# Modulation products in the mixer's gaps, a mean inside the last slab and a shorter routing chain, in a two-block network

## The chip, the cores and the metric

One core of one Trainium2 chip runs one program. The metric is the device time of one execution in microseconds (us). The engines named are PE (TensorE, matmuls), DVE (VectorE), ACT (ScalarE), POOL (GpSimd) and SP (SyncE, which only issues DMAs here).

## The reference

A first block on x (256 tokens x 1024) in float32, then a second block of four layers (swiglu, RWKV, Mamba and windowed attention). The change lies in the first block:

```
mod = (silu(c) @ w_ada + b_ada).reshape(bsz, 6, d)       # 6 x 1024 numbers: "ada1"; the second block has 72 chunks of 512, "ada2"
sh1, sc1, g1, sh2, sc2, g2 = [mod[:, j, None, :] for j in range(6)]
u = modulate(x, sh1, sc1)                                # normalise, * (1 + sc1) + sh1
mix = hybrid_mixer(u, ...)                               # rg_lru and attention, concatenated, @ w_out
x = layernorm(ALPHA * x + g1 * mix, ln1_g, ln1_b)
u2 = modulate(x, sh2, sc2)
ffn = hierarchical_moe(u2, ...)
x = layernorm(ALPHA * x + g2 * ffn, ln2_g, ln2_b)
# hierarchical_moe: 4 groups of 8 experts of width 256
g_top, g_idx = top_k(softmax(xc @ w_rg + b_rg), 1)
e_in = the 8 logits of that group
e_top, e_loc = top_k(softmax(e_in), 2); e_top = e_top / sum(e_top)
weights = g_top * e_top                                  # two experts for each token
y = sum over the two: weight * ((silu(x @ w1) * (x @ w3)) @ w2)
```

## The kernel before

Activations lie with the 1024 features on partitions, as eight tiles of 128 x 256 tokens (J = 8). A float32 matmul runs as three: each weight tile (1 MB, 128 x 2048, loaded by SP into one of four "raw" buffers, L315) is split by ACT into hi (L326) and by DVE into lo (L327), and hi*high, lo*high and hi*low are summed (mm3, L337). A raw buffer is free for the next load once lo, or what else reads it, is done; SP issues its loads in one fixed order.

Chunks of the modulation (512 numbers, two loads each) are made beside the main work, in two ways. On PE (gemv): "acc" matmuls with silu(c) as the stationary operand, a copy to "rows" on ACT, small "c" matmuls that turn the row into a column, an addition on DVE (L407). On DVE (gemv_v, L425): four products a chunk, each a 128 x 1024 multiplication by silu(c) (laid out in a tile cb by silu_rows) with a sum along the row, and a last addition of the bias (L429). ON_VECTOR says which chunks go which way. pump(n) does n PE chunks, pump(n, True) n DVE chunks, pump_parts yields after every product, need(key) does what is due.

The first block runs in this order. hybrid(): first norm, projections (the h matmuls), the recurrence and the attention (u0 to u3 by "gathered": scores, softmax with its divisions on POOL, L1356 and L1357, transposes), then the output in four slabs of w_out, out(0) to out(3) (y matmuls), the last ending tile by tile in the residual (L529). moe(): layernorm and modulate, each one call of centred: mean by eight matmuls with a constant ("bm"), U = x - mean (L576, DVE), squares on ACT (L517), their sum "st" by PE, root in ten small DVE steps (L466 to L476), broadcast "bc" by PE; then "ut" (L558, DVE) and the affine part on ACT (L560). Then router logits ("pl", lg at L1676), transposes of U ("ut" on PE) to tokens tokh and tokl, and the routing: maxima, one-hot choices, softmaxes, "own" (which of eight slots of pairs of experts a token takes), its running count "pr", "rank", one-hot matrices Gm, their transposes GT ("gt"), the gather "pg" of tokens (gh, gl), the weights "pge", and the experts' matmuls ("eh", "yp", "ya" for the scatter). mosti is the largest count of a slot; a second pass follows if it is over 128 (it isn't).

The scheduler orders each engine's instructions by priority in the order of the code; `with self.ordered()` fixes the order within a piece. silu(c1) is loaded twice before, and moe's two norms hold four chunks by `more()`:

```
more = lambda: self.pump(1, True)
with self.ordered():
    self.modulate(U, self.centred(U, more), self.col("ln1_g"), self.col("ln1_b"), self.x)
```

Of the kernel before, what the change touches and what calls it, by code (L numbers as in the profile page):

```python
# [10 lines left out]
F32 = mybir.dt.float32  # L11
# [15 lines left out]
ON_VECTOR = {"ada1": (0, 1, 2, 3, 6, 7, 8, 9), "ada2": range(2, 72)}  # L27
# [241 lines left out]
class Program:  # L269
    def __init__(self, ctx, tc, a, out):  # L270
# [4 lines left out]
        self.raw = e(tc.tile_pool(name="raw", bufs=4))  # L275
# [13 lines left out]
        self.vf = None  # L289
# [23 lines left out]
    def load(self, name, i):  # L313
        t = self.raw.tile([P, 2048], F32, name="raw")
        self.nc.sync.dma_start(t, self.a[name][i])  # L315
        return t
# [29 lines left out]
    def tr(self, out, in_, ident=None):  # L346
        self.nc.tensor.transpose(out, in_, self.k("ident") if ident is None else ident)
# [70 lines left out]
    def gemv_v(self, name, chunk, bias, out):  # L418

        nc = self.nc  # L420
        for h in range(2):
            r = self.load(name, 2 * chunk + h)
# [130 lines left out]
    def modulate(self, src, bc, A, sh, dst=None, follow=None):  # L553

        nc = self.nc
        for m in range(J):
            t = self.t1("ut")
            self.last = nc.vector.scalar_tensor_tensor(t, src[:, m, :], A[:, m:m + 1], bc, op0=OP.mult, op1=OP.mult)  # L558
            if dst is not None:
                nc.scalar.activation(dst[:, m, dst.shape[2] - T:], t, AF.Identity, bias=sh[:, m:m + 1])  # L560
                if follow:
                    follow.tile(m)
                continue
# [4 lines left out]
    def centred(self, xc, between=None):  # L568

        nc = self.nc  # L570
        bm = self.bank([P, T], "bm", self.st_tag)
        for m in range(J):
            self.mm(bm, self.k("mean"), self.x[:, m, :], m == 0, m == J - 1)
# [4 lines left out]
        if between:  # L578
            self.last = last
            with self.ordered():  # L580
                between()
            with self.ordered():
                return self.bcast_t(self.rsqrt(st, 1.0 / D, 1e-5, 2))
        return self.bcast_t(self.rsqrt(st, 1.0 / D, 1e-5, 2))
# [864 lines left out]
    def hybrid(self):  # L1449
# [3 lines left out]
        with ExitStack() as ctx:  # L1453
# [11 lines left out]
            self.silu_rows("c1", ar.tile([P, D], F32, name="cb1", tag="Z", bufs=1))  # L1465
# [7 lines left out]
            self.new_u()  # L1473
            self.modulate(xc, bc, A, M[:, 0:8])
# [108 lines left out]
            for m in range(4):  # L1583
                t = self.t1("lo")
                stt(t, cv[:, m, :], self.col("norm_lru_g", m, 1), bc, op0=OP.mult, op1=OP.mult)
                self.split(m, t)
            self.st_tag = "m"
            ys = [self.bank([P, 2, T]) for _ in range(4)]

            def out(s):  # L1590
                w = self.slab("w_out", s)
                for kk in range(2):
                    for m in range(J):
# [20 lines left out]
            out(2)  # L1614
            self.pump(1)
            out(3)
            self.st_tag = "y"


    def moe(self, follow, cb):  # L1620
# [3 lines left out]
        with ExitStack() as ctx:  # L1624
# [9 lines left out]
            nc.sync.dma_start(rb, bass.AP(tensor=rbd.tensor, offset=rbd.offset, ap=[[0, P], [1, 36]]))  # L1634
            wr = self.load("router", 0)
            U = arr("U", [P, J, T], tag="big")
            self.silu_rows("c1", ar.tile([P, D], F32, name="cb1", tag="tokh"))
            more = lambda: self.pump(1, True)
            with self.ordered():
                more()  # L1640
            with self.ordered():
                self.modulate(U, self.centred(U, more), self.col("ln1_g"), self.col("ln1_b"), self.x)
            with self.ordered():
                more()
            with self.ordered():
                bc = self.centred(U, more)
            self.need((0, 2))
            self.silu_rows("c2", cb)
            A = self.consts.tile([P, J], F32, name="A", bufs=2)
            ts(A, M[:, 32:40], 1.0, None, op0=OP.add)  # L1650
            self.modulate(U, bc, A, M[:, 24:32], U)
            for m in range(J):
                act(self.x[:, m, :], self.x[:, m, :], AF.Copy, scale=ALPHA)
# [7 lines left out]
            with self.tc.issue_after(last.ins):  # L1661
                self.pump(3)
            with self.ordered():
                more()
            tokh, tokl = arr("tokh", [P, 2, 1024], dt=F32R), arr("tokl", [P, 2, 1024], dt=F32R)
            for k in range(J):
# [5 lines left out]
                tt(tokl[:, :, c], pt, tokh[:, :, c].bitcast(F32), op=OP.subtract)  # L1672
            new = lambda name, shape: arr("r_" + name, [P, 2] + shape)
# [3 lines left out]

            def softmax(t, n, name):
                mx = new("mx" + name, [1])
                red(mx, t, axis=AX.X, op=OP.max)  # L1680
                tt(t, t, bcv(mx, n), op=OP.subtract)
                act(t, t, AF.Exp)
                red(mx, t, axis=AX.X, op=OP.add)
                nc.vector.reciprocal(mx, mx)
                tt(t, t, bcv(mx, n), op=OP.mult)
# [11 lines left out]
            softmax(lg[:, :, 0:4], 4, "g")  # L1697
            gtop, og = first_max(lg[:, :, 0:4], 4, "g")
# [9 lines left out]
            ge, sw, hh = new("ge", [8]), new("sw", [1]), new("hh", [2])  # L1708
            tt(ei, o1, o2, op=OP.add)
            red(hh, ei.rearrange("p c (h e) -> p c h e", h=2), axis=AX.X, op=OP.max)  # L1710
            tt(sw, e1, e2, op=OP.add)
# [219 lines left out]
```

## Time and profile before

| what | value |
|---|---|
| median of 3 runs | 3105.38 us (3096.54 to 3112.08) |
| the profiled execution | 3116.96 us, span 3115.1 us, mean granted clock 0.952 |
| PE busy | 2940.8 us, 94% |
| DVE, ACT, POOL busy | 74%, 52%, 6% |
| L425 products | 312, mean 1221 ns |
| chain that ended last | PE 70%, DVE 6%, ACT 3% |

A row of a timeline tells when an instruction started, how long it ran, and in brackets how long its engine had been idle before and for whom it waited. A row with x8 joins eight of one kind. Matmuls in float32 show two records for each in a row such as bm x16 (two passes), so counts of records are not always counts of instructions.

### The profile page before, as it was taken

How to read it: one execution, taken by the hardware profiler on the slowest of the kernel's cores; microseconds unless marked ns; L12 is line 12 of the kernel's file. 1: busy time of each engine (PE TensorE's matmuls, PEld its weight loads, DVE VectorE, ACT ScalarE, POOL GpSimd, SP SyncE). 2: the span in 40 equal slices, each digit the busy share in tenths (PEclk: the TensorE clock that was granted, in tenths of full speed). 3: DMA queues.
4: the chain of work that ended last, by engine and by line, in shares of the span. 5: the costliest groups of instructions: out<-in, count | busy, mean ns of one | idle time of the engine just before them, and what ended most of it. 6: DMA issues, size and time to landing. Idle time of an engine off the chain costs nothing.

```text
span 3115.1 us, 57344 instructions
## 1 busy us (share of the span) xinstructions
PE 2940.8 (94%) x23191; PEld 2721.9 (87%) x23191; DVE 2297.2 (74%) x4064; ACT 1612.9 (52%) x2779; POOL 187.1 (6%) x244
## 2 busy tenths in 40 slices
PE   7979999799889999999899999999899999899999
PEld 6867888699768899999899999997899998777899
DVE  6668888677685787776887777767776876855754
ACT  5537777444544444544775545445644544542543
POOL 1200000000410000000000000001200001400000
PEclk8979999799889999999999999999999999898999
DMA  8468888476133378584554785863487682213353
GB/s 305 167 250 324 323 324 324 180 296 257 68 113 133 132 277 323 207 316 154 199 195 157 290 293 210 322 230 138 175 298 277 241 310 95 108 60 131 147 180 135
DMA packets 95192, 674.45 MB, mean 217 GB/s; under 512 B 10759, under 2 KB 12104, under 8 KB 14664
## 3 DMA queue, kind: packets, MB, share of 16 engines
q1 hardware_dynamic: 94920, 670.71, 57.8%
q8 instruction: 184, 3.01, 0.4%
q14 instruction: 88, 0.72, 0.1%
HBM read 666.95 MB, written 3.72 MB: 215 GB/s over the span
## 4 chain that ended last, share of the span: by engine, by line
PE 70%; DVE 6%; ACT 3%; POOL 1%; issue 1%; DMA 0%; POOLq 0%; DVEq 0%; ACTq 0%; SPq 0%
PE h L337 40%; PE y L337 16%; PE ea L337 3%; DVE lo L327 1%; PE pk L337 1%; PE py L337 1%; PE st L337 1%; ACT hi L326 1%; PE pg L337 1%; PE pw L337 1%; PE hb L337 1%; DVE ut L558 1%; PE z L337 1%; PE zg L337 1%; PE pa L337 1%
## 5 line engine op out<-in xcount | busy, mean ns | idle before, releaser
L327 DVE TENSOR_TENSOR lo<-raw,hi 128x1024 fp32r<-128x1024 f32 x897 | 1085.2, 1226 | 375.4 <-ACT hi L326 372.5
L326 ACT CAST hi<-raw 128x1024 fp32r<-128x1024 f32 x897 | 928.1, 1050 | 634.3 <-PE h L337 284.9
L337 PE MATMUL h<-uh,hi 128*128 128x256 f32 x3552 | 1023.6, 288 | 20.2 <-ACT hi L326 11.6
L337 PE MATMUL h<-uh,lo 128*128 128x256 f32 x3552 | 1016.5, 287 | 11.4 <-DVE lo L327 11.4
L337 PE MATMUL h<-ul,hi 128*128 128x256 f32 x3552 | 1016.8, 286 | 9.0 <-DVE ul L358 9.0
L337 PEld LDWEIGHTS h<-uh,hi 128*128 128x128 f32 x3552 | 682.9, 192 | 32.8 <-ACT hi L326 14.0
L337 PEld LDWEIGHTS h<-uh,lo 128*128 128x128 f32 x3552 | 682.6, 192 | 16.1 <-DVE lo L327 13.2
L337 PEld LDWEIGHTS h<-ul,hi 128*128 128x128 f32 x3552 | 683.2, 192 | 14.4 <-DVE ul L358 10.4
L425 DVE SCALAR_TENSOR_TENSOR raw<-raw,cb 128x1024 f32<-128x1024 f32 x312 | 375.1, 1221 | 42.2 <-DMA raw<-in_ada 41.7
L337 PE MATMUL y<-gh,hi 128*128 128x256 f32 x1408 | 395.7, 281 | 0.0
L337 PE MATMUL y<-gh,lo 128*128 128x256 f32 x1408 | 395.6, 281 | 0.0
L337 PE MATMUL y<-gl,hi 128*128 128x256 f32 x1408 | 395.5, 281 | 0.0
L337 PEld LDWEIGHTS y<-gh,hi 128*128 128x128 f32 x1408 | 265.6, 189 | 0.0
L337 PEld LDWEIGHTS y<-gl,hi 128*128 128x128 f32 x1408 | 265.5, 189 | 0.0
L337 PEld LDWEIGHTS y<-gh,lo 128*128 128x128 f32 x1408 | 265.1, 188 | 0.0
L521 POOL TENSOR_TENSOR sq<-sq 128x256 f32<-128x256 f32 x60 | 49.5, 824 | 2234.0 <-ACT sq L517 1705.5
L357 ACT CAST gh<-g 128x256 fp32r<-128x256 f32 x176 | 71.3, 406 | 155.1 <-DVE g L627 151.0
L625 ACT ACTIVATE sa<-h 128x256 f32<-128x256 f32 x160 | 60.8, 380 | 140.6 <-PE h L337 140.0
L337 PE MATMUL eh<-hi,gh 128*128 128x512 f32 x256 | 104.5, 408 | 0.7 <-ACT hi L326 0.7
L337 PE MATMUL eh<-lo,gh 128*128 128x512 f32 x256 | 103.2, 403 | 1.8 <-DVE lo L327 1.8
L337 PE MATMUL eh<-hi,gl 128*128 128x512 f32 x256 | 101.9, 398 | 0.0
L337 PE MATMUL ea<-uh,hi 128*128 128x258 f32 x312 | 89.9, 297 | 2.0 <-ACT uh L221 2.0
(489 smaller groups left out, 4266.3 us busy)
## 6 DMA issues: line engine op xcount, KB each, us to landing
raw<-in_ffn_in SPq DMA_DIRECT2D x176, 1024.0 KB, 4.9
raw<-in_ada SPq DMA_DIRECT2D x168, 1024.0 KB, 5.1
raw<-in_w SPq DMA_DIRECT2D x96, 1024.0 KB, 4.8
raw<-in_ffn_out SPq DMA_DIRECT2D x88, 1024.0 KB, 7.1
raw<-in_rw SPq DMA_DIRECT2D x32, 1024.0 KB, 4.8
raw<-in_mb_in SPq DMA_DIRECT2D x24, 1024.0 KB, 4.9
raw<-in_w_in SPq DMA_DIRECT2D x10, 1024.0 KB, 5.5
raw<-in_mb_out SPq DMA_DIRECT2D x8, 1024.0 KB, 4.7
```

Source lines behind the costliest of these rows:

```text
L326: self.nc.scalar.copy(hi, r[:, c])
L327: self.nc.vector.tensor_tensor(lo, r[:, c], hi.bitcast(F32), op=OP.subtract)
L337: self.pe = self.nc.tensor.matmul(out, lhs, rhs, start=start, stop=stop, skip_group_check=True)
L357: self.nc.scalar.copy(uh[:, m, :], t)
L425: nc.vector.scalar_tensor_tensor(w, w, 1.0, self.cb, op0=OP.mult, op1=OP.mult, accum_out=out[:, 2 * h + j:2 * h + j + 1])
L521: self.nc.gpsimd.tensor_tensor(self.acc, self.acc, sq, op=OP.add)
L558: self.last = nc.vector.scalar_tensor_tensor(t, src[:, m, :], A[:, m:m + 1], bc, op0=OP.mult, op1=OP.mult)
L625: nc.scalar.activation(sa, a, AF.Silu, bias=bias)
```

## The change

- ada2 chunks 0 and 1 go from PE to DVE. Of the DVE chunks due in moe, five (ada1 6 to 9, ada2 0) are made in hybrid() as single products at eleven places, `some(n)`; ada2 1 to 3 in moe as 12 single products. The four products at the experts' end are gone. silu(c1) stays in the permanent tile; loads of these chunks in moe go to two buffers of their own ("side"). The PE chunks ada1 10 and 11 go to between the norms and behind the token transposes.
- The mean's matmuls of the first norm stand inside out(3), two tiles behind the residual. The factor ALPHA on x goes into the affine step (L560) and the next norm's constants.
- own is made from the raw logits; softmax weights (`weights`) and the largest count (`count`) are made beside the first gather. GT comes after the gather; gl of the first gather is cast on DVE. SP's load of the count stands earlier.

```diff
-ON_VECTOR = {"ada1": (0, 1, 2, 3, 6, 7, 8, 9), "ada2": range(2, 72)}
+ON_VECTOR = {"ada1": (0, 1, 2, 3, 6, 7, 8, 9), "ada2": range(72)}
...
+    def mean_of(self, m):
+        if m == 0:
+            self.bm = self.bank([P, T], "bm", self.st_tag)
+        if m >= 0:
+            self.mm(self.bm, self.k("mean"), self.x[:, m, :], m == 0, m == J - 1)
...
+            ahead = self.pump_parts(5)
...
             project(2)
             S[2] = weigh(2)
+            some(1)
             gathered(0, S[0])
             project(3)
+            some(2)
             S[3] = weigh(3)
+            some(1)
             gathered(1, S[1])
+            some(1)
...
                         if s == 3 and kk == 1:
                             self.residual(m, y, M[:, 16:24], None)
+                            self.mean_of(m - 2)
...
-            out(0)
+            out(0, 2)
             gathered(2, S[2])
             self.pump(1)
-            out(1)
+            out(1, 3)
             gathered(3, S[3])
             self.pump(1)
+            some(3)
...
-            out(2)
-            self.pump(1)
-            out(3)
+            out(2, 2)
             self.st_tag = "y"
+            self.silu_rows("c2", ar.tile([P, D], F32, name="cb2", tag="zr", bufs=1))
+            some(2)
+            out(3, 2)
...
+            self.modulate(U, self.centred(U, lambda: some(3)), self.col("ln1_g"), ab, self.x, scale=ALPHA)
+            self.pump(1)
+            with self.ordered():
+                some(3)
+            self.modulate(U, self.centred(U, lambda: (some(3), self.flush()), ALPHA), A, M[:, 24:32], U)
+            with self.ordered():
+                some(3)
...
-            softmax(lg[:, :, 0:4], 4, "g")
-            gtop, og = first_max(lg[:, :, 0:4], 4, "g")
+            gmax, og = first_max(lg[:, :, 0:4], 4, "g")
...
-            softmax(ei, 8, "e")
             e1, o1 = first_max(ei, 8, "1")
-            stt(ei, o1, -2.0, ei, op0=OP.mult, op1=OP.add)
+            stt(ei, o1, -3e38, ei, op0=OP.mult, op1=OP.add)
...
-                    nc.scalar.copy(gl[:, k], pg[:, 1])
+                    (nc.vector.tensor_copy if start else nc.scalar.copy)(gl[:, k], pg[:, 1])
+                if start:
+                    weights()
+                    mosti.append(count())
```

What the order of the instructions makes of it. First DVE from the last residuals to the first norm's root, before (mod_91 is ada1's result, mod_87 ada2's):

```order
L529 SCALAR_TENSOR_TENSOR x<-y,mod_91,x 128x256 x8
L407 TENSOR_TENSOR mod_91<-c_1571,cols 128x4
L425 SCALAR_TENSOR_TENSOR raw,mod_91<-raw,cb_1568 128x1024 x4
L429 TENSOR_TENSOR mod_91<-mod_91,cols 128x4
L576 TENSOR_TENSOR U<-x,bm 128x256 x8
L425 SCALAR_TENSOR_TENSOR raw,mod_91<-raw,cb_1568 128x1024 x4
L429 TENSOR_TENSOR mod_91<-mod_91,cols 128x4
L466 TENSOR_SCALAR rsv<-st 128x2
```

and after:

```order
L529 SCALAR_TENSOR_TENSOR x<-y,mod_91,x 128x256
L429 TENSOR_TENSOR mod_87<-mod_87,cols 128x4
L529 SCALAR_TENSOR_TENSOR x<-y,mod_91,x 128x256 x6
L1675 TENSOR_SCALAR ab<-cols 128x8
L1676 TENSOR_SCALAR A<-mod_91 128x8
L529 SCALAR_TENSOR_TENSOR x<-y,mod_91,x 128x256
L577 TENSOR_TENSOR U<-x,bm 128x256 x8
L425 SCALAR_TENSOR_TENSOR raw,mod_87<-raw,cb 128x1024 x2
L466 TENSOR_SCALAR rsv<-st 128x2
L467 TENSOR_SCALAR rst<-rsv 128x2
L468 TENSOR_SCALAR rsy<-rst 128x2
L470 TENSOR_TENSOR rst<-rsy 128x2
```

Two of the chunks' products stood in front of U by fours; now U follows the last residual, and two products stand behind it, a third within the root (behind the last row shown, L472).

DVE in the mixer, from the second unit's scores to the first root, before:

```order
L1354 RECIPROCAL sm<-sm 128x4
L1577 TENSOR_TENSOR cv<-cv,yg 128x256
L1348 TENSOR_SCALAR nm<-nm 128x4
L1577 TENSOR_TENSOR cv<-cv,yg 128x256
L327 TENSOR_TENSOR lo<-raw,hi 128x1024
L1354 RECIPROCAL sm<-sm 128x4
L327 TENSOR_TENSOR lo<-raw,hi 128x1024
L1577 TENSOR_TENSOR cv<-cv,yg 128x256 x2
L327 TENSOR_TENSOR lo<-raw,hi 128x1024
```

and after:

```order
L425 SCALAR_TENSOR_TENSOR raw,mod_91<-raw,cb 128x1024
L1356 TENSOR_SCALAR nm<-nm 128x4
L1595 TENSOR_TENSOR cv<-cv,yg 128x256 x2
L425 SCALAR_TENSOR_TENSOR raw,mod_91<-raw,cb 128x1024
L1362 RECIPROCAL sm<-sm 128x4
L327 TENSOR_TENSOR lo<-raw,hi 128x1024
L425 SCALAR_TENSOR_TENSOR raw,mod_91<-raw,cb 128x1024
L1362 RECIPROCAL sm<-sm 128x4
L425 SCALAR_TENSOR_TENSOR raw,mod_91<-raw,cb 128x1024
L1595 TENSOR_TENSOR cv<-cv,yg 128x256 x2
L429 TENSOR_TENSOR mod_91<-mod_91,cols 128x4
L327 TENSOR_TENSOR lo<-raw,hi 128x1024
```

Three lo of weight slabs stood between the attention's steps; now two, and four products (one more chunk's stand further ahead).

PE behind the last accumulation to the gather, before:

```order
L337 MATMUL acc<-raw,s_c_85 32x512 x8
L337 MATMUL c_1879<-kc,rows 128x1 x4
L337 MATMUL pr<-r_own,kc 128x8 x5
L347 MATMUL gt<-kc,Gm 128x128 x4
L337 MATMUL pg<-Gm,tokh 128x256 x2
L337 MATMUL pg<-Gm,tokl 128x256 x2
```

and after:

```order
L337 MATMUL acc<-raw,s_c_83 32x512 x8
L337 MATMUL pr<-r_own,kc 128x8 x3
L337 MATMUL pg<-Gm,tokh 128x256 x3
L337 MATMUL pg<-Gm,tokl 128x256 x2
L337 MATMUL pg<-Gm,tokh 128x256
L337 MATMUL pg<-Gm,tokl 128x256 x2
L337 MATMUL eh<-hi,gh 128x512
L337 MATMUL pg<-Gm,tokh 128x256 x2
L337 MATMUL pg<-Gm,tokl 128x256 x2
```

gt stood in front of the first pg; now pg follows pr, and the first expert matmuls (eh) stand among the pg.

## Rows read from the trace of the kernel before

**Rows 1.** Windows: stretch, busy PE, PEld, DVE, ACT, POOL, clock, DMA, GB/s.

```profile
100.00:120.00 20.00, 18.60 (x149) 16.45 (x148) 13.21 (x26) 17.42 (x35) 14.36 (x13) 1.00 0.34 116
...
400.00:420.00 20.00, 20.00 (x106) 16.93 (x105) 19.00 (x27) 13.62 (x19) 0.00 (x0) 1.00 0.78 278
```

**Rows 2.** Finer windows, after the mixer's last matmul and in the first norm.

```profile
169.00:175.00 6.00, 1.92 (x9) 1.33 (x8) 5.96 (x14) 0.45 (x2) 0.00 (x0) 1.00 0.36 127
...
175.00:182.00 7.00, 6.83 (x32) 6.75 (x32) 6.62 (x16) 2.28 (x7) 0.00 (x0) 0.52 0.73 277
```

**Rows 3.** Timeline of PE: start, us, op, tiles, count, idle before.

```profile
160.47 0.39 PE L337 MATMUL y<-uh,hi 128*128 128x256 f32 x1
...
168.48 0.28 PE L337 MATMUL y<-uh,lo 128*128 128x256 f32 x1
...
168.59 2.32 PE L337 MATMUL bm<-x,kc 128*128 128x256 f32 x10
...
175.02 6.83 PE L337 MATMUL st<-kc,sq 128*128 128x1 f32 x32 [4.10 <-ACT sq L517]
...
193.51 5.34 PE L337 MATMUL st<-kc,sq 128*128 128x1 f32 x32 [2.52 <-ACT sq L517]
...
210.84 0.91 PE L337 MATMUL pl<-raw,U 128*128 128x36 f32 x4
...
223.23 1.94 PE L337 MATMUL acc<-raw,s_c 128*32 128x512 f32 x8 [0.76 <-DMA raw<-in_ada]
...
227.60 2.28 PE L337 MATMUL pr<-r_own,kc 128*128 128x8 f32 x10
...
230.62 1.24 PE L347 MATMUL gt<-kc,Gm 128*128 128x128 f32 x4 [0.74 <-DVE mosti L1734]
...
231.78 0.80 PE L337 MATMUL pg<-Gm,tokh 128*128 128x256 f32 x2
...
249.11 0.39 PE L337 MATMUL eh<-lo,gh 128*128 128x512 f32 x1
```

**Rows 4.** Timeline of DVE: norms and routing.

```profile
169.26 1.22 DVE L425 SCALAR_TENSOR_TENSOR raw<-raw,cb 128x1024 f32<-128x1024 f32 x1
...
174.04 2.73 DVE L576 TENSOR_TENSOR U<-x,bm 128x256 f32<-128x256 f32 x8
...
184.69 3.22 DVE L558 SCALAR_TENSOR_TENSOR ut<-U,cols,bc 128x256 f32<-128x256 f32 x8 [0.86 <-PE bc L347]
...
192.60 2.73 DVE L576 TENSOR_TENSOR U<-x,bm 128x256 f32<-128x256 f32 x8
...
198.68 1.22 DVE L425 SCALAR_TENSOR_TENSOR raw<-raw,cb 128x1024 f32<-128x1024 f32 x1
...
202.88 3.22 DVE L558 SCALAR_TENSOR_TENSOR ut<-U,A,bc 128x256 f32<-128x256 f32 x8 [0.92 <-PE bc L347]
...
211.83 0.22 DVE L1676 TENSOR_TENSOR r_lg<-pl,rb 128x72 f32<-128x72 f32 x1
...
225.29 0.17 DVE L1722 TENSOR_TENSOR r_own<-r_og,r_hh 128x16 f32<-128x16 f32 x1
```

**Rows 5.** Timeline of ACT, end of the first gather.

```profile
238.64 0.38 ACT L1756 CAST gl<-pg 128x256 fp32r<-128x256 f32 x1
```

**Rows 6.** Timeline of POOL and DVE in the mixer's attention.

```profile
98.44 0.93 POOL L1357 TENSOR_SCALAR S<-S,sm 128x256 f32<-128x256 f32 x1
...
102.22 1.22 DVE L327 TENSOR_TENSOR lo<-raw,hi 128x1024 fp32r<-128x1024 f32 x1
...
102.23 2.00 POOL L1357 TENSOR_SCALAR S<-S,sm 128x256 f32<-128x256 f32 x1
```

**Rows 7.** Timeline of SP: DMA issues near the mixer's last weight slab.

```profile
146.30 0.33 SPq L315 DMA_DIRECT2D raw<-in_w_out  x1
```

**Rows 8.** Timeline of DVE and PE at the experts' end.

```profile
551.85 1.22 DVE L425 SCALAR_TENSOR_TENSOR raw<-raw,cb 128x1024 f32<-128x1024 f32 x1
...
553.53 0.77 PE L337 MATMUL ya<-GT,yhl 128*128 128x256 f32 x4 [2.78 <-DVE x L529]
```

More of the change, by code (lines that the diff above doesn't have):

```diff
@@ L421, in gemv_v @@
         for h in range(2):
-            r = self.load(name, 2 * chunk + h)
+            r = self.load(name, 2 * chunk + h, self.side)
             for j in range(2):
@@ L566, in modulate, with centred @@
                                            op0=OP.add, op1=OP.subtract)
-    def centred(self, xc, between=None):
+    def centred(self, xc, between=None, scale=1.0):
         nc = self.nc
-        bm = self.bank([P, T], "bm", self.st_tag)
-        for m in range(J):
-            self.mm(bm, self.k("mean"), self.x[:, m, :], m == 0, m == J - 1)
+        for m in range(0 if self.bm is None else J, J):
+            self.mean_of(m)
+        bm, self.bm = self.bm, None
         st = self.stat()
@@ L1473, in hybrid, with some @@
             self.new_u()
+            ahead = self.pump_parts(5)
+            def some(n):
+                for _ in range(n):
+                    next(ahead)
             self.modulate(xc, bc, A, M[:, 0:8])
@@ L1586, in hybrid, with out @@
                 self.split(m, t)
+            some(1)
             self.st_tag = "m"
             ys = [self.bank([P, 2, T]) for _ in range(4)]
-            def out(s):
+            def out(s, then=0):
                 w = self.slab("w_out", s)
+                some(then)
                 for kk in range(2):
@@ L1660, in moe, with tokens @@
                                    k == 0 and th == 0, k == J - 1)
[L1661 to L1664, printed above, removed]
             tokh, tokl = arr("tokh", [P, 2, 1024], dt=F32R), arr("tokl", [P, 2, 1024], dt=F32R)
-            for k in range(J):
+            def tokens(k):
                 pt = self.bank([P, 2, P], "ut", "h")
@@ L1723, in moe @@
                hh[:, :, None, :].to_broadcast([P, 2, 4, 2]), op=OP.mult)
-            pr = self.bank([P, 3, 8], "pr", "m")
+            for k in range(J):
+                tokens(k)
+            with self.tc.issue_after(self.tr_last.ins):
+                self.pump(1)
+            pr = self.bank([P, 2, 8], "pr", "m")
             tri, ones = self.k("mtri")[:, 0:P], self.k("ones")
@@ L1728, in moe, with count, weights, gather @@
             self.mm(pr[:, 1, :], tri, own[:, 1, :], False, True)
[L1729 to L1736 removed]
+            self.last = nc.vector.tensor_copy(rank, pr)
+            mosti = []
+            def count():
+                pm = self.bank([P, 8], "pm", "m")
+                self.mm(pm, ones, own[:, 0, :], True, False)
+                self.mm(pm, ones, own[:, 1, :], False, True)
+                most, n = arr("most", [P, 1]), arr("mosti", [P, 1], dt=I32)
+                red(most, pm, axis=AX.X, op=OP.max)
+                nc.vector.tensor_copy(n, most)
+                return n
+            def weights():
+                lgg = lg[:, :, 0:4]
+                tt(lgg, lgg, bcv(gmax, 4), op=OP.subtract)
+                act(lgg, lgg, AF.Exp)
+                tt(e2, e2, e1, op=OP.subtract)
+                act(e2, e2, AF.Exp)
+                red(e1, lgg, axis=AX.X, op=OP.add)
+                ts(sw, e2, 1.0, None, op0=OP.add)
+                tt(e1, e1, sw, op=OP.mult)
+                nc.vector.reciprocal(e1, e1)
+                tt(e2, e2, e1, op=OP.mult)
+                tt(o1, o1, bcv(e1, 8), op=OP.mult)
+                tt(o2, o2, bcv(e2, 8), op=OP.mult)
+                tt(ge, o1, o2, op=OP.add)
+            def gather(g, start=False):
                 Gm, GT = arr("Gm", [P, 2, 2, P], dt=F32R), arr("GT", [P, 2, T], 2, F32R)
@@ L1820, in experts @@
                     ts(rank, rank, -128.0 * window, None, op0=OP.add)
-                G, later, hd, GT = gather(0), None, None, None
+                G, later, hd, GT = gather(0, not window), None, None, None
                 for e in range(33):
@@ L1852, in moe @@
             self.need((0, 3))
-            count = nc.values_load(mosti[0:1, 0:1], min_val=0, max_val=T)
-            with self.tc.If(count > P):
+            most = nc.values_load(mosti[0][0:1, 0:1], min_val=0, max_val=T)
+            with self.tc.If(most > P):
                 experts(1)
+            self.side = None
             self.st_tag = "m"
```

100 lines of the change are left out of this document (38 added, 62 removed).

## The prediction

> **What bounds the kernel now.** I read the windows first. In [rows 1] the columns to see are PE's busy time and the clock. The experts (400 to 420 us) keep PE busy for 20.00 of 20 us at clock 1.00: that stage is as long as its matmuls, and nothing the change does before it shortens it; it can only begin earlier. The mixer at 100 to 120 us is nearly as full on PE (18.60), while DVE has 13.21 busy there: some room for products, if they can be slipped in without making PE wait. What lies between is different: in [rows 2] a PE that waits, and a clock of 0.52 (mostly the lower level) when it works again at 175 us, after the idle 169 to 175. From the end of the last mixer matmul (168.48 + 0.28 = 168.76 us, T0 below) to the 24th expert matmul (249.11 + 0.39 = 249.50, second and last rows of [rows 3]) 80.7 us pass in which one chain of small steps sets the end. The chain of waits as a view reaches back only to the branch behind the experts, so I followed this stretch by hand through PE and DVE [rows 3, 4].
>
> Sums are made against the profiled execution (3116.96 us); the median of the three runs is 3105.38, 11.6 us lower, and I carry the difference over to it.
>
> **Norms: products out, mean in the slab.** Before, four products (1.15 us apart) run between the residual and U, four beside the statistics, four between the norms, four in the second norm, 16 in all [rows 4]. U waits for the first four: it starts at 174.04, T0 + 5.28, though the mean's matmuls end at 168.59 + 2.32 = 170.9. After, the order has U right behind the last residual, and all but the last mean matmuls stand in front of the last y: one residual (about 0.4) and some four mean matmuls (0.23 each by the ten of [rows 3]) give U at about T0 + 1.25. The products that remain are 12: two between U and the root, one within the root (its ten steps are 0.2 us apart, so that one costs its whole 1.15), three before the second U, and the same again, with the last three before the logits.
> From U to ut it was 10.65 us (174.04 to 184.69); statistics at 6.83 us for 32 at the lower level. Since PE now idles only some 3 us before them they may run faster: if they merely follow the squares, ut comes at T0 + 10.3; if as before, with the extra product, at T0 + 13.2. I take 11.6. To the second U: 3.22 for ut, three products instead of four, so 6.75 instead of 7.91: T0 + 18.4 (before 23.84). Second norm: the products no longer end after the statistics (before 198.68 + 1.2 = 199.9 against 193.51 + 5.34 = 198.85, 1.1 us), one stands in the root (+1.15): 10.3 as before (192.60 to 202.88), ut at T0 + 28.7. From there to the logits (8.95 before) PE is the limit: pl with transposes between, to 210.84 + 0.91; fewer transposes come in between, and the three products that stand in front of lg fit under it. 8.2: logits at T0 + 36.9, before 43.07. Saved 6.2; from 3.5 (lower level in both norms) to 9.5 (upper level in both).
>
> **Routing.** From logits to own it was 13.6 us (211.83 to 225.46). Four chained softmax parts, of which two exponentials on ACT, and waits for c matmuls and tokl's casts on DVE go out. After, about 21 steps 0.2 us apart (4.65 with the wider ones) and eight tokl subtractions (0.34 each) that DVE takes in between, plus some wait for tokh: 8.1 us. From own to the first gather matmul it was 6.3 us (225.46 to 231.78): c, pr x10 in 2.28, rank, Gm, then gt x4 in 1.24 in front of pg [rows 3]. After: pr has six of ten passes (1.4), gt is behind, all four Gm must be there: 4.5. The eight remaining acc matmuls stand before pr (1.94 for such a group) but lie beside the DVE chain. Saved 13.6 + 6.3 - 8.1 - 4.5 = 7.3. If ACT's hi of the second weight slab, which now sits between tokh's casts, waits for its load, 2 us of it are lost.
>
> **Gather to the 24th expert matmul.** Before 17.7 (231.78 to 249.50): all of pg, then pge, then 24 eh, the first of them with a wait for lo. After, gt (1.24) and a second small count fall into this stretch, but eh stand among pg as soon as a gh is there; the eight casts of gl go from ACT (0.38 each [rows 5], 3.0 in all) to DVE, which has lost four products there, so that hi and lo come sooner. If none of that helps it is 17.7 + 1.24 + 1.3 for the count and the longer queue, 20.2; if ACT's 3.0 and the waits for the first eh go, and gt fits into gaps, 15.5. I take 17.0: saved 0.7 (from -2.5 to +2.2). SP's new place for the count (a register load after six expert loads instead of at the end) has 90 expert loads queued behind it; the count is ready with the first gather, before the seventh of these loads can have a free buffer, so I put it at nothing; if that cover fails, each us of lateness is one of PE's.
> Sum of the stretch: 6.2 + 7.3 + 0.7 = 14.2 saved, from 9 to 19.
>
> **Mixer.** It takes 20 products (23 us of DVE) and their ten 1 MB loads more, and loses one group of acc on PE in front of the last slab (-1.9). Eight of them lie before the first root, where DVE is fullest: 9.2 us against the 6.8 that DVE has left from 100 to 120 us and some before 100. And they meet POOL: its 128x256 step takes 0.93 alone and 2.00 when it starts with a lo on DVE (102.23 and 102.22 in [rows 6]), 1.07 more. A product has lo's shape and time. Four stand between the attention's steps (the order of DVE in the mixer shows it), in place of one of three lo: at 1.07 each POOL's chain is some 3 to 4 us longer, of which PE waits for a part only since the slab's h matmuls are there to fill.
> The Trainium skill (SBUF — State Buffer, "SBUF: two separate sides") says that a DVE instruction with two SBUF inputs and a GpSimd instruction that reads SBUF exclude one another for the whole instruction; the 2.00 against 0.93 agrees. By that rule all four products cost POOL a full 1.1 us each, 4.3 together; if products were harmless there the mixer's term would be about 2 us smaller.
> Then a lo between the second root and its use (+1.2) and the last slab's load, issued at 146.30 before [rows 7], now with two more 1 MB loads close to it; y of that slab starts at 160.47 (the first row of [rows 3]), 14.2 us after the issue, so a few us of lateness are covered. Together the mixer is 3.5 us longer; bounds -2 (all hidden, acc gone) and +8 (POOL's 4.3, lo's 1.2, DVE's 2.4 too much).
>
> **Tail.** Four products, the last at 551.85, stand between the last steps of the experts and the residuals: PE's ya waits 2.78 for DVE [rows 8]. Without them the residuals begin 2.1 us earlier, and two small steps (0.3) go: -2.4, bounds -1 and -2.8. The second block's own work is not touched.
>
> **Sum.** -14.2 + 3.5 - 2.4 = -13.1: 3103.9 against the profiled run, 3092.3 against the median. I say 3092; its own range is 3084 to 3099.
>
> **Rivals.** (A) The clock: fewer idle us let the norms and the gather run at the upper level. For it: 1.00 at 169 to 175 [rows 2], so the level falls only after the wait for U, and that wait shrinks from 4.10 (behind the statistics) by more than half. Against: pl, small transposes and one-column statistics keep gaps between them. Then -19 + 2 - 2.4, about -19: 3086. (B) The mixer gives it back: the PE there is full, each late root or late slab goes to the end one for one, and the stretch saves its lower 9: -9 + 8 - 1, about -2: 3103. (C) Slower than before: the four raw buffers. The chunks' loads stand in SP's order in front of the mixer's slabs, and a load waits until a product has freed a buffer; the product waits its turn on DVE behind lo and the roots. For the last slab the slack is 14.2 us less some 6 for landing, hi and lo; beyond 8 us of lateness each us is PE's. It decides from 11.4 us lost in all, the stretch's lower 9 with the tail's 2.4; two slabs each 9 us past their slack make 18, so +7: 3112. Against it: the slab that waits longest in the order waits for a product of a chunk already half done. That the change does not do what it says is not a case: the order has the products where the diff puts them.
>
> **Numbers.** Forecast 0.53, A 0.27, B 0.14, C 0.06. The three runs lie 15.5 us apart, so within 0.5% (15.5 us) is no change. Faster by more than that (under 3090): A, and the forecast's own lower third, 0.27 x 0.8 + 0.53 x 0.3 = 0.38; slower by more (over 3121): half of C, 0.03, and 0.02 for a scattered median; same 0.57. Range 3079 to 3106: A's lower bound to most of B.
>
> **What would show it.** U about 1.3 us behind the last y; statistics near 4 or near 7 us tell A from the forecast; own 8 us after lg; no gt in front of pg, eh between pg; no PE idle before the tail's ya; in the mixer the first y at most 4 us later, the last y by 173, POOL's 128x256 steps at 2 us beside products. Wrong if the last y comes over 8 us later than T0, or if PE waits for raw loads in the experts' first slabs.

## The result, and the profile after

The median of 15 runs each is 3084.42 us (3075.42 to 3097.10) after and 3107.49 us (3096.54 to 3115.61) before: 23.1 us less, ratio 0.9929, 95% interval [0.9914, 0.9945]. I had said 13 less, in a range that reaches to 3079; the median came out 1.6 below the 3086 of rival A. A second series of both kernels, on another chip (e9), gives 17.1 less, ratio 0.9945 [0.9924, 0.9965].

The spans of the two profiled executions lie 37.2 us apart (3115.1 and 3077.9), which is more than the change did: behind the join (PE's restart with the mean behind the experts) the code is the same, and this rest took 2552.5 us before and 2538.3 after. In the twelve kernels below it took from 2537 to 2551, and e6 and e10, which are one kernel, differ there by 12.8 (2537.1 and 2549.8, at mean granted clocks of 0.958 and 0.954 over the whole execution). So what follows is read from marks ahead of the join, in us, each from one profiled execution; e3 to e8 and e12 were run only that once. e6 and e10 also show how far marks can be trusted: T0 differs by 2.0 and a stretch by up to 0.8.

| kernel | last y ends (T0) | T0 to lg | lg to own | own to first pg | first pg to 24th eh | 24th eh to last yp | last yp to join | join |
|---|---|---|---|---|---|---|---|---|
| before | 168.8 | 43.1 | 13.6 | 6.3 | 17.7 | 299.6 | 13.4 | 562.6 |
| after | 171.8 | 35.2 | 7.3 | 3.3 | 13.1 | 298.6 | 10.3 | 539.6 |
| e1 products back | 168.4 | 43.5 | 6.7 | 9.2 | 17.7 | 298.7 | 13.4 | 557.5 |
| e2 routing back | 172.3 | 35.3 | 12.5 | 4.3 | 12.8 | 297.4 | 10.3 | 544.9 |
| e3 mean behind | 171.7 | 35.9 | 7.5 | 3.0 | 13.1 | 298.7 | 10.3 | 540.2 |
| e4 before, fillers | 168.9 | 42.6 | 13.1 | 3.3 | 17.1 | 299.7 | 14.3 | 559.0 |
| e5 two chunks on PE | 172.7 | 38.9 | 8.0 | 15.4 | 16.7 | 299.2 | 10.0 | 560.9 |
| e6 out of attention | 167.2 | 36.2 | 7.2 | 4.7 | 14.0 | 298.8 | 10.1 | 538.1 |
| e7 products 2, 4, 2, 4 | 170.0 | 39.0 | 7.3 | 6.1 | 13.5 | 298.5 | 10.6 | 544.8 |
| e8 fillers in routing | 170.1 | 37.4 | 8.2 | 5.8 | 12.1 | 298.6 | 10.1 | 542.2 |
| e9 after again | 169.6 | 35.4 | 7.5 | 3.3 | 13.2 | 298.7 | 10.1 | 537.7 |
| e10 e6 again | 169.2 | 36.1 | 7.3 | 3.9 | 13.4 | 298.9 | 10.2 | 539.1 |
| e11 e6, three fillers | 173.3 | 36.0 | 8.0 | 2.9 | 12.1 | 298.6 | 10.2 | 541.0 |
| e12 no side buffers | 172.5 | 36.0 | 8.0 | 4.4 | 14.6 | 299.4 | 10.4 | 545.4 |

From before to after the join comes 23.0 us earlier: mixer +3.0, norms -7.9, routing -9.3 (6.3 and 3.0), gather -4.6, experts -1.0, tail -3.2 (each rounded by itself). That this equals the median's difference is partly chance: T0 alone moves by 2 us between executions of one code.

PE after, in the columns of [rows 3]:

```profile
171.51 0.29 PE L337 MATMUL y<-uh,lo 128*128 128x256 f32 x1
...
173.02 1.06 PE L337 MATMUL acc<-raw,s_c 128*32 128x512 f32 x8
174.12 4.10 PE L337 MATMUL st<-kc,sq 128*128 128x1 f32 x32
...
190.34 3.73 PE L337 MATMUL st<-kc,sq 128*128 128x1 f32 x32 [0.18 <-ACT sq L517]
...
212.63 3.00 PE L337 MATMUL acc<-raw,s_c 128*32 128x512 f32 x16
215.56 0.83 PE L337 MATMUL pr<-r_own,kc 128*128 128x8 f32 x6
217.65 0.59 PE L337 MATMUL pg<-Gm,tokh 128*128 128x256 f32 x3 [1.25 <-DVE Gm L1778]
...
219.00 0.80 PE L337 MATMUL eh<-hi,gh 128*128 128x512 f32 x1
...
230.35 0.40 PE L337 MATMUL eh<-lo,gh 128*128 128x512 f32 x1
```

The 32 of st take 4.10 and 3.73 instead of 6.83 and 5.34, with no wait of 4.10 ahead of the first: U comes four us sooner behind T0, and acc of a modulation chunk fills what is left. pr is six records in 0.83 instead of ten in 2.28, no gt stands in front of pg, the first eh comes 1.35 behind the first pg, and the 24th (230.35) 19 us earlier than before (249.11 in [rows 3]).

DVE after, in the columns of [rows 4]:

```profile
173.13 2.74 DVE L577 TENSOR_TENSOR U<-x,bm 128x256 f32<-128x256 f32 x8 [0.81 <-PE bm L337]
...
179.41 1.22 DVE L425 SCALAR_TENSOR_TENSOR raw<-raw,cb 128x1024 f32<-128x1024 f32 x1
...
182.16 3.22 DVE L558 SCALAR_TENSOR_TENSOR ut<-U,cols,bc 128x256 f32<-128x256 f32 x8 [0.86 <-PE bc L347]
...
189.41 2.73 DVE L577 TENSOR_TENSOR U<-x,bm 128x256 f32<-128x256 f32 x8 [0.53 <-PE bm L337]
...
198.43 3.22 DVE L558 SCALAR_TENSOR_TENSOR ut<-U,A,bc 128x256 f32<-128x256 f32 x8 [0.93 <-PE bc L347]
...
207.01 0.23 DVE L1704 TENSOR_TENSOR r_lg<-pl,rb 128x72 f32<-128x72 f32 x1 [1.93 <-PE pl L337]
...
214.18 0.17 DVE L1732 TENSOR_TENSOR r_own<-r_og,r_hh 128x16 f32<-128x16 f32 x1
```

U follows T0 (171.51 + 0.29) by 1.33 and waits 0.81 for the mean. The product at 179.41 stands within the root, as the order said.

POOL after, against [rows 6], and PE behind it:

```profile
99.59 2.62 POOL L1364 TENSOR_SCALAR S<-S,sm 128x128 f32<-128x128 f32 x1 [72.50 <-DVE nm L1356]
...
106.29 2.70 POOL L1365 TENSOR_SCALAR S<-S,sm 128x256 f32<-128x256 f32 x1
...
109.55 0.92 POOL L1365 TENSOR_SCALAR S<-S,sm 128x256 f32<-128x256 f32 x1
```

```profile
121.89 0.33 PE L347 MATMUL pt<-kc,S 128*128 128x128 f32 x1 [1.07 <-POOL S L1364]
122.79 0.69 PE L347 MATMUL pt<-kc,S 128*128 128x128 f32 x2 [0.57 <-POOL S L1365]
```

The same step takes 2.70 beside a lo and a product, 0.92 alone, and PE now waits for POOL (1.07 and 0.57; before, one wait of 0.23). The trace agrees with the Trainium skill's rule that the prediction weighed (SBUF — State Buffer, "SBUF: two separate sides"): POOL's 16 steps of the two first units add up to 22.4 us instead of 17.5, 4.9 more, where the prediction's estimate was 4.3; a single step can cost more than the 2.00 I took. DVE then waits 5.35 us for the first root's statistics (1.76 before).

The tail, against [rows 8]:

```profile
531.51 3.84 PE L337 MATMUL ya<-GT,yhl 128*128 128x256 f32 x24 [0.56 <-DVE x L529]
539.59 5.15 PE L337 MATMUL bm<-x,kc 128*128 128x256 f32 x16 [4.24 <-PEq L1894]
```

The wait of ya for DVE is 0.56 instead of 2.78.

### The profile page after: what moved, and what is told of

Its sections match the earlier page's. It is cut to its first block, busy times and chain, and to the rows that moved or that the text cites. A ratio compares the mean times of both kernels' runs of the same rounds, so it can differ in the third digit from the quotient of the medians.

```text
span 3077.9 us, 57213 instructions
## 1 busy us (share of the span) xinstructions
PE 2914.1 (95%) x23143; PEld 2704.6 (88%) x23143; DVE 2305.1 (75%) x4081; ACT 1606.6 (52%) x2761; POOL 191.3 (6%) x244
## 4 chain that ended last, share of the span: by engine, by line
PE 69%; DVE 7%; ACT 3%; issue 1%; POOL 1%; DMA 0%; POOLq 0%; DVEq 0%; ACTq 0%
PE h L337 40%; PE y L337 16%; PE ea L337 3%; DVE lo L327 1%; PE py L337 1%; PE pk L337 1%; ACT hi L326 1%; PE st L337 1%; DVE ut L558 1%; PE pw L337 1%; PE hb L337 1%; PE pg L337 1%; PE zg L337 1%; PE z L337 1%; PE pa L337 1%
## 5 line engine op out<-in xcount | busy, mean ns | idle before, releaser
L337 PEld LDWEIGHTS h<-uh,hi 128*128 128x128 f32 x3552 | 684.8, 193 | 29.9 <-ACT hi L326 12.7
L425 DVE SCALAR_TENSOR_TENSOR raw<-raw,cb 128x1024 f32<-128x1024 f32 x320 | 385.0, 1221 | 48.1 <-DMA raw<-in_ada 47.3
```

Source lines behind the costliest of these rows:

```text
L337: self.pe = self.nc.tensor.matmul(out, lhs, rhs, start=start, stop=stop, skip_group_check=True)
L425: nc.vector.scalar_tensor_tensor(w, w, 1.0, self.cb, op0=OP.mult, op1=OP.mult, accum_out=out[:, 2 * h + j:2 * h + j + 1])
```

## The experiments

In e1 and e2 one part is undone in the changed kernel, so that each also shows the other part alone on the kernel before.

**e1: products and PE chunks where they were.**

```diff
-ON_VECTOR = {..., "ada2": range(72)}
+ON_VECTOR = {..., "ada2": range(2, 72)}
...
 # in short: hybrid() without some(), pump(1) between out(2) and out(3) again; moe() with more() at
 # four places, pump(3) and more() behind pl, pump(1, True) at the experts' end, no side buffers
```

> The changed kernel with the products of the modulation and its PE chunks where the kernel before has them (four before U, beside the statistics, between the norms and in the second norm, four in the gather, four at the experts' end; no products in the mixer); mean in the slab and the short routing stay. Theory T (the three parts, products, routing and gather, each give their own share, and add): the mixer's last matmul 2.5 to 3.5 us earlier than in the changed kernel (171.8 us), so 168 to 169.5; logits at T0 + 41.5 to 43.5 instead of 35.2; the tail from the last yp to the join 13.2 to 13.6 us instead of 10.3; the join (restart of PE at the mean behind the experts) at 548 to 552 us, ratio to before 0.9955 to 0.997. Rival R (the shorter routing with the gather is nearly all of it, since the statistics hide the products): join at 541 to 545, ratio 0.993 to 0.995.

Ratio 0.9995 [0.9978, 1.0011]; the join at 557.5. Theory T's stretches hold up to the logits and in the tail, but the loss is larger than either theory said: by the marks the short routing alone (the mean in the slab gives nothing here, U is at T0 + 5.3 as before) is worth 5.0 of the 23.0 us, and in time no gain is seen. The chain is short (own 6.7 us behind lg), but pr has to wait:

```profile
222.16 1.92 PE L337 MATMUL acc<-raw,s_c 128*32 128x512 f32 x16
224.79 1.05 PE L337 MATMUL c<-kc,rows 128*128 128x1 f32 x8 [0.70 <-ACT rows L401]
225.70 0.81 PE L337 MATMUL pr<-r_own,kc 128*128 128x8 f32 x6
...
230.65 0.80 PE L337 MATMUL pg<-Gm,tokh 128*128 128x256 f32 x2 [1.52 <-DVE gl L1779]
...
233.60 0.79 PE L337 MATMUL pg<-Gm,tokh 128*128 128x256 f32 x2 [0.88 <-DVE gl L1779]
```

The last chunk's acc and c end at 225.8, 7 us behind own (218.6), and pr stands behind them. In the gather, PE waits for gl, which now is DVE's, behind the four products that follow Gm (1.52 and 0.88). Two edits that look independent meet here: the cast moved to DVE makes PE wait 2.4 us where DVE still has its products, and not in the changed kernel.

**e2: routing and first gather as before.**

```diff
-            gmax, og = first_max(lg[:, :, 0:4], 4, "g")
+            softmax(lg[:, :, 0:4], 4, "g")
+            gtop, og = first_max(lg[:, :, 0:4], 4, "g")
...
 # in short: likewise for the eight; token transposes ahead of lg in the code; third count, rank and
 # mosti ahead of the gather, gt in front of pg, gl on ACT
```

> The changed kernel with the routing and the first gather as the kernel before has them (both softmaxes in the chain, third count and largest count before the gather, gt in front of pg, gl cast on ACT). Theory T: nothing moves up to the logits (T0 + 35.2), then logits to own 10 to 12 us instead of 7.3, own to the first pg 5 to 6.5 instead of 3.3, first pg to the 24th eh 15 to 18 instead of 13.1; join at 546 to 551 us, ratio to before 0.995 to 0.997. Rival R (norms and products are nearly all of it, the chain was covered by the transposes on PE and ACT): logits to the first pg at most 1.5 us longer than in the changed kernel, join at 540 to 543.

Ratio 0.9979 [0.9958, 0.9999]; the join at 544.9, just under T's 546. Of T, lg to own is as long as said (12.5, even 0.5 over), the rest is wrong: with gt in front and gl on ACT own to the 24th eh takes 17.0 together, 16.4 after. So these two edits gave that stretch some 0.6, and the gather's 4.6 us came with the other part, the products, chunks and side buffers. Undoing the routing costs 5.3 us, and the other part by itself gives 17.7; with e1's 5.0 that is 22.7 of 23.0, so by the marks the parts add. The times do not confirm it: e2's ratio makes it 6.5 us faster than the kernel before, 13 by the end of its interval, and not 17.7. In its profile the missing part lies behind the join (2550.6 us there, 2538.3 after), where the code is the same; its ten runs have a median granted clock of 0.952, the kernel before beside it 0.955. Whether the edit or chance lowered that clock is open.

**e3: the mean behind the last y.**

```diff
-                            self.mean_of(m - 2)
-                if s == 3:
-                    self.mean_of(J - 2)
-                    self.mean_of(J - 1)
```

> The changed kernel with the mean's eight matmuls behind the last y instead of inside the last slab. Theory T (the mean in the slab gives what its matmuls take behind the last y, less what they take inside): the last y 1 to 1.6 us earlier (170.2 to 170.8), U at T0 + 2.8 to 3.8 instead of T0 + 1.3, so U 0.3 to 1.5 us later in all; the statistics as long as in the changed kernel (3.7 to 4.3 us for 32). Rival (x arrives late and sets U): U unchanged in all.

T's numbers failed: the last y stays (171.7), U is at T0 + 1.8, 0.4 later in all, the join 0.6 later. That is less than one profile can tell, so the rival (U unchanged) stands. The edit also moved little: the scheduler still put four of the eight matmuls (bm x8 at 169.45) in front of the last y, against five after; before it was three:

```profile
166.86 1.54 PE L337 MATMUL bm<-x,kc 128*128 128x256 f32 x6
```

So U's 4 us (T0 + 5.28 to T0 + 1.33) came from the products leaving the place in front of it, and the mean's new place is worth half a microsecond at most.

**e4: the kernel before, with matmuls of no use where PE waits in the norms.**

```diff
+        if self.fill:                             # set to [8, 5] in moe()
+            f = self.bank([P, T], "fill", "y")
+            for i in range(self.fill.pop(0)):
+                self.mm(f, self.k("mean"), self.x[:, i % 7, :], True, True)
```

> The kernel before with 8 and 5 matmuls of no use on PE between the mean and the statistics of the two norms, where PE waits 4.10 and 2.52 us. Theory C (the lower clock in the norms comes from PE's waits): the 32 records of the first statistics take 3.7 to 4.5 us instead of 6.83, granted clock in that stretch over 0.9 instead of 0.52; U to ut gets only 0.5 us shorter, since the four products end at T0 + 12.6 and the root waits for them; join 0 to 2 us earlier. Rival (one-column matmuls themselves lower the clock): 6 us or more for the 32, clock below 0.7.

```profile
170.90 3.62 PE L337 MATMUL fill<-x,kc 128*128 128x256 f32 x16
175.16 3.73 PE L337 MATMUL st<-kc,sq 128*128 128x1 f32 x32 [0.65 <-ACT sq L517]
```

Theory C holds: 3.73 at a granted clock of 1.00 for the 32 records that took 6.83 [rows 3], so the slow records there came from the idle PE ahead of them and not from what they compute. The root waits for the products, so U to ut gets only 0.4 shorter, as expected. Not expected: own to the first pg falls from 6.3 to 3.3, and acc, c and pr run at the upper level there too (granted clock 0.95 at 224 to 228 instead of 0.50). The join comes 3.6 earlier, in one execution, by an edit that only adds matmuls of no use.

**e5: two of the chunks on PE again.**

```diff
-ON_VECTOR = {..., "ada2": range(72)}
+ON_VECTOR = {..., "ada2": range(2, 72)}
...
-                self.pump(1)        # behind the token transposes
+                self.pump(3)
 # and eight some() fewer, as told below
```

> The changed kernel with ada2 0 and 1 on PE again, behind the token transposes with ada1 11 (three chunks there instead of one); the eight products that this saves DVE are gone from hybrid (four) and moe (four, two products at each of its four places). Theory P (the short routing is worth its full time only because the PE chunks left: with three of them PE, not DVE's chain, ends last before pr): own to the first pg 6 to 9 us instead of 3.3; first pg to the 24th eh 13 to 15. Rival D (the gain there is the four products that no longer follow Gm on DVE): own to the first pg at most 4.5 us, the rest unchanged. Either way the last y is 0 to 1.5 us earlier and the norms 1 to 2.5 us shorter.

```profile
218.17 3.64 PE L337 MATMUL acc<-raw,s_c 128*32 128x512 f32 x16
222.51 1.86 PE L337 MATMUL c<-kc,rows 128*128 128x1 f32 x8 [0.71 <-ACT rows L401]
224.31 3.64 PE L337 MATMUL acc<-raw,s_c 128*32 128x512 f32 x16
228.66 1.86 PE L337 MATMUL c<-kc,rows 128*128 128x1 f32 x8 [0.71 <-ACT rows L401]
230.45 1.93 PE L337 MATMUL acc<-raw,s_c 128*32 128x512 f32 x8
232.31 1.45 PE L337 MATMUL pr<-r_own,kc 128*128 128x8 f32 x6
```

Theory P, at twice its price: each chunk is 16 records of acc (3.64), a wait of 0.7 for ACT's copy and eight c (1.86), all at the lower level, and pr is the last in the queue, 13 us behind own. Two small chunks at this place cost 12 us, and the join is at 560.9, nearly that of the kernel before. The gather's 16.7 missed the 13 to 15: half of the third chunk's acc falls into it, and the first expert load is issued only at 226.30. The expectation for mixer and norms failed too (no earlier y, norms 3.7 longer): acc now stands between st, and acc and c in front of bc.

**e6 and e10: products out of the attention.**

```diff
             project(0)
+            some(2)
             project(1)
+            some(2)
...
             project(6)
+            some(2)
...
-            some(1)                 # and the others around weigh and gathered, and behind the root
```

> The changed kernel with the five products of the attention's places and the one behind the first root moved: six into the projections (50 to 90 us), where DVE waits and POOL is idle. Theory S (products beside POOL's division steps lengthen both, and the 3.0 us by which the mixer is longer come from there): POOL's 16 steps of the two first units take 19 to 22 us in all instead of 22.5 and start earlier; first y at 128.5 to 130.5 instead of 132.3, last y at 168.5 to 170 instead of 171.8; join 2 to 3.5 us earlier than 539.6. Rival L (the slabs' later loads make it): first y within 0.7 us of 132.3.

> e6's kernel, timed. Theory S (the mixer without products beside POOL ends 3 to 4.6 us earlier; what the norms and the gather gave back in e6, 3.1 us, came with the lower clock of that execution and not with the edit): median 2 to 4.5 us below the changed kernel's on this chip. Rival (it is given back in every execution, since the loads of the norms' chunks then meet the expert weights): within 1.5 us of it.

```profile
116.13 0.60 POOL L1364 TENSOR_SCALAR S<-S,sm 128x128 f32<-128x128 f32 x1 [4.83 <-DVE sm L1362]
```

POOL's 16 steps add up to 17.5 us (22.4 after, 17.5 before), so products do lengthen them, by more than S said. But the first y stays at 132.2, as L said, though not for L's reason, since the first slab's load is issued earlier here (93.37 instead of 103.08): at 40 to 60 us PE is busy 13.88 of 20 instead of 15.97, beside a DVE that now is busy 19.19. From first to last y it takes 35.0 us instead of 39.5, and of the 4.6 by which T0 comes earlier the norms, the routing and the gather give back 3.1. Timed, e10 has ratio 0.9939 [0.9918, 0.9960] and e9 0.9945 [0.9924, 0.9965] to before: no difference, as the rival said. The six products were not free at either of the two places tried.

**e7: two products in each norm, four behind.**

```diff
-            ... self.centred(U, lambda: some(3)) ...
+            ... self.centred(U, lambda: some(2)) ...
-                some(3)
+                some(4)
 # the same in the second norm
```

> The changed kernel with two products in each norm and four behind each affine step, instead of three and three. Theory (the product inside the root's ten steps is on the path, the one behind ut is not while PE's mean or pl is late): U to ut 7.7 to 8.1 us instead of 9.0 in both norms; ut to the second U 7.2 to 7.8 instead of 7.25 (four products end 0.6 us behind the mean); ut to the logits unchanged; logits at T0 + 33.2 to 34, join 1.2 to 2 us earlier. Rival: the scheduler's other order lets the statistics or the accumulation delay the root, logits not over 0.5 us earlier.

The theory fell: logits at T0 + 39.0 instead of 35.2, join 5.2 later.

```profile
177.64 1.92 PE L337 MATMUL acc<-raw,s_c 128*32 128x512 f32 x2 [1.64 <-DMA raw<-in_ada]
...
184.46 6.31 PE L337 MATMUL bm<-x,kc 128*128 128x256 f32 x16
```

```profile
175.17 1.23 DVE L425 SCALAR_TENSOR_TENSOR raw<-raw,cb 128x1024 f32<-128x1024 f32 x1 [1.14 <-DMA raw<-in_ada]
...
190.81 2.74 DVE L577 TENSOR_TENSOR U<-x,bm 128x256 f32<-128x256 f32 x8 [2.64 <-PE bm L337]
```

The products arrive late (1.14 for the DMA), PE's acc waits for its load in front of bm (1.64), and the second U waits 2.64 for bm. Here taking a product out of the root only moved the wait, to the loads and to what stands in front of bm.

**e8 and e11: fillers in the routing.**

```diff
+                if k > 0:                          # e11: k in (4, 5, 6), one matmul, on e6's kernel
+                    f = self.bank([P, T], "fill", "y")
+                    with self.tc.issue_after(self.tr_last.ins):
+                        for i in range(2):
+                            self.mm(f, self.k("mean"), self.x[:, i, :], True, True)
```

> The changed kernel with 14 matmuls of no use on PE, two behind each pair of token transposes from the second on, where PE waits for DVE and ACT. Theory C (what runs at the lower clock there does so because PE waited): granted clock from the logits to the first pg over 0.85 instead of 0.50 to 0.74, first pg to the 24th eh 11.5 to 12.3 us instead of 13.1; the fillers that stand in front of transposes cost 0 to 1.5 us before own. Rival (transposes and small matmuls hold the clock down whatever is between): clock under 0.7 there, gather 13 us or more.

> e6's kernel with three matmuls of no use on PE, one behind each of the last pairs but one of token transposes, where PE waits 0.5 to 1.0 us for DVE. Theory C: granted clock between the logits and the first pg 0.1 or more above e10's, pr x6 at 0.8 to 0.9 us (1.45 in e6), first pg to the 24th eh 12 to 13; median 0 to 2 us below e10's. Rival: PE's queue reaches acc and pr later by the fillers' 1.4 to 2.8 us, and DVE waits for pr: median 0 to 2 us above e10's.

Windows after, and then of e8:

```profile
212.00:218.00 6.00, 4.75 (x29) 2.01 (x28) 3.89 (x24) 2.16 (x5) 0.00 (x0) 0.76 0.40 130
218.00:224.00 6.00, 6.00 (x32) 5.42 (x31) 4.80 (x7) 2.81 (x7) 0.00 (x0) 0.72 0.79 298
```

```profile
212.00:218.00 6.00, 6.00 (x34) 4.51 (x37) 3.35 (x19) 2.54 (x6) 0.00 (x0) 0.86 0.00 0
218.00:224.00 6.00, 4.64 (x37) 2.96 (x30) 3.69 (x9) 1.33 (x4) 0.00 (x0) 1.00 0.70 262
```

The clock rises as theory C says (0.86 and 1.00 instead of 0.76 and 0.72; from the logits to the first pg 0.78, short of the 0.85 expected), and the gather runs at 1.00 throughout and takes 12.1 us in both kernels, against 13.1 after and 13.4 in e10. But own to the first pg is 2.5 us longer in e8, with the fillers in PE's queue. e11's ratio is 0.9947 [0.9926, 0.9967], no gain on e10 either.

**e9: the changed kernel once more.** Its edit is none.

> The changed kernel itself, so that the next two stand beside it on one chip. Ratio to before 0.991 to 0.9945; in its profile the last y between 169.9 and 172.7 us and the first pg to the 24th eh between 12.5 and 14 us: that is what the same code showed in the other kernels of this study.

The marks between T0 and the 24th eh came out within 0.5 us of the first profile's; the mixer differs by 2.2 us, so that the last y (169.6) falls just below its range. With e6 and e10, whose stretches differ by up to 0.8, this says that a difference of well over 1 us in a stretch behind T0 can be read from one profile, and one of 2 us in T0 can't.

**e12: no side buffers.**

```diff
-            self.side = ctx.enter_context(self.tc.tile_pool(name="side", bufs=2))
```

> The changed kernel without the two side buffers: the loads of the chunks in the norms use the four raw buffers again, with the expert weights behind them. Theory E (the first gather is short because the first expert weights are there and split before it): first expert load issued at 203 us or later instead of 194.9, PE then waits for hi or lo between the first eh, first pg to the 24th eh 14.5 to 18 instead of 13.1. Rival (the weights were early enough in any case, and the gather is short by the clock and by DVE's missing four products): 12.5 to 14.

```profile
208.97 48.47 SPq L315 DMA_DIRECT2D raw<-in_w  x14
```

```profile
220.97 2.35 DVE L327 TENSOR_TENSOR lo<-raw,hi 128x1024 fp32r<-128x1024 f32 x2
```

```profile
223.71 0.80 PE L337 MATMUL pg<-Gm,tokh 128*128 128x256 f32 x2 [0.84 <-DVE gl L1789]
```

The first expert load is issued at 208.97 (194.89 after, 222.53 before), own to pg and gather take 4.4 and 14.6, the join is 5.8 later, of which 0.7 are the mixer's. The gather is at the lower edge of theory E, but not by the wait that E named: three hi still run ahead of the gather; PE waits 0.84 for gl, which stands on DVE behind two lo (one in the changed kernel), and its matmuls take 0.6 longer at a granted clock of 0.77 instead of 0.87. So the side buffers are worth some 1.5 us of the gather, part of it by the clock. Weights as late as before are not tested by this edit.

## Why the prediction was right, and where it was too small

The median lies in the stated range because rival A lies in it, not because the sum came out: every term was better than said (mixer 0.5, norms 1.7, routing 2.0, gather 3.9, experts 1.0, tail 0.8), so nothing cancelled. In time it is at the lower edge of the forecast's own 3084 to 3099; as a difference, 23.1, it lies just beyond that, and I had given the larger chance (0.57) to a change of no more than 15.5 us. The 17.1 of the second series would lie within the forecast's own range.

- Mixer: 3.5 forecast, 3.0 measured, but 0.8 in the other profile of the same code (e9), and from 0.8 to 3.8 in the kernels that change only what lies behind the slabs; so the sign is shown, and the close match is luck. That products lengthen POOL's steps is shown (22.4 instead of 17.5, and 17.5 again in e6); that the mixer's delay comes from there is argued from PE's waits for POOL, and e6, where the first y came no earlier, does not confirm it.
- Norms: 6.2 forecast, 7.9 measured. U at T0 + 1.33 (1.25 said). The mean's matmuls were counted at 0.23 each, which is one of a matmul's two records, and three of the eight stood in front of the last y before as well; the product that left, not the mean's place, made U early (e3). I took ut between the two clock levels (11.6); it came at 10.4, as A had it. e4 shows that the idle PE ahead of the statistics sets their level. The second norm from U to ut, put at 10.3, took 9.0.
- Routing: 7.3 forecast, 9.3 measured: lg to own 7.3 (8.1 said), own to pg 3.3 (4.5 said). The mechanism was told in part wrongly: I gave the saving to the shorter chain and put the acc in front of pr at nothing, as lying "beside the DVE chain". pr starts 1.2 us behind own, when acc is done. By e1 and e2 the chain is worth 5 us, and by e1 and e5 (pr 7.1 and 12.7 us behind own) what stands in front of pr decides how much of it is seen.
- Gather, the step that failed: "I take 17.0: saved 0.7", with 15.5 as the best case, if ACT's 3.0 and the waits for the first eh go. Measured 13.1, outside the bounds. The windows of the gather, first of before and then of after (columns as in [rows 1]):

```profile
231.80:249.50 17.70, 15.55 (x66) 12.84 (x66) 11.81 (x21) 11.88 (x24) 0.00 (x0) 0.77 0.60 223
```

```profile
217.65:230.75 13.10, 13.10 (x73) 11.58 (x74) 10.41 (x20) 6.52 (x14) 0.00 (x0) 0.87 0.71 273
```

PE's idle 2.15 us are gone, and its matmuls take 2.45 less at a clock of 0.87 instead of 0.77, though the four of gt are now among them; ACT is busy for 6.52 instead of 11.88. The longest of the waits before was for lo of the first expert weights:

```profile
242.55 0.50 PE L337 MATMUL eh<-lo,gh 128*128 128x512 f32 x1 [1.26 <-DVE lo L327]
```

The first expert loads, before and then after, and ACT's timeline after say why it went:

```profile
222.53 3.02 SPq L315 DMA_DIRECT2D raw<-in_w  x2
```

```profile
194.89 20.06 SPq L315 DMA_DIRECT2D raw<-in_w  x3
```

```profile
204.02 1.99 ACT L326 CAST hi<-raw 128x1024 fp32r<-128x1024 f32 x2
211.88 1.05 ACT L326 CAST hi<-raw 128x1024 fp32r<-128x1024 f32 x1 [0.54 <-DMA raw<-in_w]
222.68 1.06 ACT L326 CAST hi<-raw 128x1024 fp32r<-128x1024 f32 x1 [0.74 <-PE eh L337]
```

Three hi casts ran ahead of the gather, since the expert weights were issued 28 us earlier than before, and the next one waits for PE. I had looked at what the new SP order puts in front of the expert loads and not at when the buffers become free. And gl's move to DVE, which I counted for it, gave next to nothing (e2). That the weights took PE's waits away is seen in e2, where gl is back on ACT, the first expert load is issued at 195.48 and PE waits for nothing in the gather. So the sum left out two things: the weights' earlier arrival and the clock. What each would give alone is not settled: e12 gives back 1.5 of both together, and the fillers of e8 win another 1.0 by the clock.
- Tail: 2.4 forecast, 3.2 measured; ya itself also ran faster (24 records in 3.84 instead of 4.74). The experts, put at nothing, took 1.0 less; why is open.
- Rival A is the outcome in size, and its cause is shown in part: fillers alone raise the clock and shorten what follows (e4, e8). But A gave all to the clock, and the gather's waits went with the weights; from the logits to own the clock is even lower after (0.50 instead of 0.75). Rivals B and C did not come: the last slab's load was later (150.81 against 146.30) and cost nothing to be seen apart from the mixer's 3.0.

## What to carry to other kernels

Before shortening a chain of small steps, look at what its result queues behind: here the chain was worth 5 us, and two chunks of small matmuls put in front of its result on PE cost 12 (e5). Ask of every moved load when its buffer is freed, since that sets when the next stage's weights are there. And read a change of a per cent from marks between which the code differs and from repeated times, not from two spans: the unchanged rest moved by 14 us here. Where marks and times disagree, as in e2, say so.

## What the runs showed of the hardware

- Matmuls without use in PE's waits made later, useful ones faster: 32 one-column records in 3.73 instead of 6.83 us (e4), the gather in 12.1 instead of 13.1 (e8). On the kernel before, the join came 3.6 us earlier with them, in one execution (e4); in the changed kernel they won nothing (join 2.6 later in e8, no gain in time in e11).
- A 128x128 POOL step of 0.60 us took up to 2.62 beside DVE's 128x1024 instructions with two inputs from SBUF, more than the one such instruction of 1.22 us that I had priced.
